# The second group's weight sums queued one group later, their rows 4 KB

## The chip, the cores and the metric

The kernel runs on one core of a Trainium2 chip. A core has a tensor engine (PE, whose weight loads the profile lists as PEld), a vector engine (DVE), a scalar engine (ACT), a general engine (POOL, GpSimd) and a sync engine (SP) that here only issues transfers. Sixteen DMA engines move the data. The metric is the device time of one execution, in microseconds (us), as the median of several runs.

## What is computed

One transformer block on 1024 positions of width 1024, all in fp32: a mixer (stick-breaking attention beside a gated linear recurrence) and an MLP with a squared relu. The change touches how the MLP's weights are prepared.

```python
def sq_relu_mlp(h, w_up, w_down):
    return jnp.square(jax.nn.relu(h @ w_up)) @ w_down

def reference(x, norm1_g, w_in, ..., norm2_g, w_up, w_down):
    h = rms_norm(x, norm1_g[l])
    x = x + hybrid_mixer(h, w_in[l], ..., w_out[l])
    h = rms_norm(x, norm2_g[l])
    x = x + sq_relu_mlp(h, w_up[l], w_down[l])
```

`w_up` is 1024 x 4096 and `w_down` 4096 x 1024.

## The kernel before

Each fp32 matmul is made of three matmuls on operands split in a high and a low part (`mmc`, L633): ACT rounds the high part (`split`, L544), DVE or POOL subtracts it from the operand (`lo_part`, L60). So each operand tile costs a pass of ACT and one of DVE or POOL before PE can use it.

The program has three parts in time. First the input projections, the recurrence and attention, whose pieces stand in a list, `ORDER`. Then the output projection with the second norm. Then the MLP, in two groups of 2048 hidden units: `up_group(0)`, `down_group(0)`, `up_group(1)`, `down_group(1)` (L837). In each, matrix products of 2 x 2 blocks are made with seven block products in place of eight (Winograd's form of Strassen's scheme): `p1` to `p7`. This needs sums of weight blocks. A group of the MLP has 14 products of 96 matmuls, 1344 in all.

In `up_group(g)` the first loop over j (`a` tiles, one load for each j) makes two block products in one go. A loop on `rs` tiles follows (`p6` and `p7`; POOL adds two loaded halves, L698), then one on `rt` tiles (`p4`; one load for two j, first operand `t4`), then one on `ru` and `rv` tiles: four loads for each j, and POOL adds them (L737). I call this last loop the `ru` loop. In `down_group(g)` a product runs over four k. It loads one tile for each k, `p1`, `p3`, `p7` and `p2`, or two that POOL adds (`rp`, `qp`, L767), `p5`, `p6` and `p4`. Before each product some tiles of the activations `U` are combined, on POOL or DVE (`s1` to `s4`, L798 to L817). The order of the products is p1, p5, p6, p3, p7, p2, p4.

The sums that several steps share are made by DMA, from DRAM to DRAM. `weight_sum(n)` (L136) copies 2 MB of `w_up` or `w_down` to a half of `sum_u` or `sum_d` (n % 4 of 0 or 1), or adds 2 MB to it on the way (`accum_op`, n % 4 of 2 or 3; called an accumulate below, the other a plain copy). There are 16: n = 0 to 3 and 4 to 7 for `sum_u` and `sum_d` of group 0, queued in attention (the Y entries of `ORDER`), 8 to 11 and 12 to 15 for those of group 1, queued in `up_group(0)` and `down_group(0)`. All are issued by POOL, in line with its arithmetic: what stands behind such an issue on POOL comes after it.

What fixes the order: the program is built with a scheduler that simulates the time of each instruction and chooses from it each engine's order (`schedule_with_timeline_sim=True`, L870). At run time each engine works its list in order. `issue_after(marked[0])` keeps a sum behind the POOL addition that was last marked with `mark`. The loads go through six `raws` buffers (`raw`, L529), so a load waits till the tile six before it has been used. The consumers of group 1's sums are the loads of `SU` (L697, L735, L736) and of `SD` (`rd`, L792).

Of the kernel before, what the change touches and what calls it, by code (L numbers as in the profile page):

```python
# [14 lines left out]
ALU = mybir.AluOpType  # L15
# [28 lines left out]
def kernel(ctx, tc, x, norm1_g, w_in, conv_w, conv_b, w_rg, b_rg, w_ig, b_ig,  # L44
                             lam, q_norm_g, k_norm_g, w_out, norm2_g, w_up, w_down, out):
    nc = tc.nc
# [89 lines left out]
    def weight_sum(n):  # L136
        m, g = (("u", 0), ("d", 0), ("u", 1), ("d", 1))[n // 4]
        i, k, dst = ((1, 0, 0), (0, 1, 1), (0, 0, 0), (1, 1, 1))[n % 4] if m == "u" else ((1, 1, 0), (0, 0, 1), (0, 1, 0), (1, 0, 1))[n % 4]

        def rows(w):  # L140
            return w.rearrange("j p c -> (j p) c") if len(w.shape) == 3 else w


        f = 16 * g + 8 * i
        src = rows(w_up[k, f:f + 8] if m == "u" else w_down[k, f * P:(f + 8) * P])
        with tc.issue_after(marked[0]):
            nc.gpsimd.dma_start(rows(sums[m, g][dst]), src, max_dma_last_dim=2048, **({"accum_op": ALU.add} if n % 4 > 1 else {}))

    left1 = ExitStack()
    hp = pool(left1, "hT")  # L150
# [493 lines left out]
    def up_group(g):  # L644
# [25 lines left out]
        for j in range(9):  # L670
            cur = None
            if j < 8:
                st = station(f"a{g}{j}", two(w_up[:, 16 * g + j]))
                ps = out_bank(f"p1_{g}{j}")
                mm4(ps, st, 0, b11)
                nc.scalar.copy(U[:, j, 2], ps)
                cur = (ps, st)
            if held is not None:
                ps, st = held
                mm4(ps, st, 1, b21, False)  # L680
                relu2(j - 1, 0, ps)
            held = cur

        for u in range(2):
# [9 lines left out]
        for j in range(8):  # L694
            r = raw(f"rs{g}{j}")
            nc.sync.dma_start(r[:, 0], w_up[1, 16 * g + 8 + j])
            nc.sync.dma_start(r[:, 1], SU[0, j])  # L697
            mark(nc.gpsimd.tensor_tensor(r[:, 0], r[:, 0], r[:, 1], **add))  # L698
            if g == 0 and j % 4 == 0:
                weight_sum(8 + j // 4)  # L700
            st = split(nc.vector, pair(stp, f"s{g}{j}"), r)
            ps = out_bank(f"p6_{g}{j}")
            mm4(ps, st, 0, t2)
            nc.vector.tensor_tensor(U[:, j, 2], U[:, j, 2], ps, **sub)
            ps = out_bank(f"p7_{g}{j}")
            mm4(ps, st, 1, t3)
            nc.vector.tensor_tensor(U[:, j, 3], ps, U[:, j, 2], **add)
# [4 lines left out]
            nc.vector.tensor_tensor(r, hb(1, 0, u), hb(1, 1, u), **sub)  # L712
            t4.append(split(lo_eng(), pair(mvp, f"t4{g}{u}"), r))
        for j in range(8):
            if g == 0 and j % 4 == 2:
                weight_sum(10 + j // 4)
            if j % 2 == 0:
                st = station(f"t{g}{j}", two(w_up[1, 16 * g + 8 + j:16 * g + 10 + j]))
            ps = out_bank(f"p4_{g}{j}")
            mm4(ps, st, j % 2, t4)  # L720
            nc.vector.tensor_tensor(U[:, j, 1], ps, U[:, j, 3], **sub)  # L721
            relu2(j, 1)
# [30 lines left out]
    def down_group(g):  # L753
        SD = sums["d", g]

        def banks4(q, name):
            return [bank(q[t], [512], f"{name}{g}{t}") for t in range(4)]

        def product(name, pss, src, unit, start):

            for k in range(0, 8, 2):
                r = raw(f"r{name}{g}{k}")
                nc.sync.dma_start(r, src[0](k))
                if len(src) > 1:
                    q = raw(f"q{name}{g}{k}")
                    nc.sync.dma_start(q, src[1](k))
                    mark(nc.gpsimd.tensor_tensor(r, r, q, **add))  # L767
                    if g == 0 and name != "p4" and k % 4 == 0:
                        weight_sum(12 + (2 if name == "p6" else 0) + k // 4)
                mv = split(nc.vector, pair(mvp, f"{name}{g}{k}"), r)  # L770
                st = split(nc.vector if len(src) > 1 else lo_eng(), pair(stp, f"{name}{g}{k}"), unit(k))
                for a in range(2):
                    for t in range(4):
                        c = slice(t * P, t * P + P)
                        mmc(pss[t], st[0][:, a, c], st[1][:, a, c], mv[0][:, a], mv[1][:, a], start and k + a == 0, k + a == 7)

        def acc(pss, rows, n, scale, last=False):

            for t in range(4):
                r = 4 * rows + t  # L780
                xs = x1[:, r, 512 * n:512 * n + 512]
                nc.vector.scalar_tensor_tensor(xs, pss[t], scale[:, r:r + 1], xs, op0=ALU.mult, op1=ALU.add)
                if last and g == 1:
                    nc.sync.dma_start(out[r * P:(r + 1) * P, 512 * n:512 * n + 512], xs)

        def wd(i, n):
            def src(k):
                f = (16 * g + 8 * i + k) * P
                return w_down[n, f:f + 2 * P].rearrange("(a p) c -> p a c", p=P)
            return src  # L790

        def rd(i):  # L792
            return lambda k: SD[i, k * P:(k + 2) * P].rearrange("(a p) c -> p a c", p=P)

        def unit(q):
            return lambda k: U[:, k:k + 2, q]

        def s1(k):  # L798
            u = U[:, k:k + 2]
            (nc.gpsimd, nc.vector)[k // 2 % 2].tensor_tensor(u[:, :, 2], u[:, :, 2], u[:, :, 3], **sub)  # L800
            return u[:, :, 2]

        def s2(k):
            u = U[:, k:k + 2]
            (nc.gpsimd, nc.vector)[k // 2 % 2].tensor_tensor(u[:, :, 2], u[:, :, 2], u[:, :, 0], **sub)
            return u[:, :, 2]

        def s4(k):
            u = U[:, k:k + 2]
            r = raw(f"s4{g}{k}")  # L810
            mark(nc.gpsimd.tensor_tensor(r, u[:, :, 1], u[:, :, 2], **add))
            return r

        def s3(k):
            u = U[:, k:k + 2]
            nc.vector.scalar_tensor_tensor(u[:, :, 2], u[:, :, 2], -1.0, u[:, :, 3], op0=ALU.mult, op1=ALU.subtract)
            return u[:, :, 2]  # L817

        pa = banks4(QA, "pa")
        product("p1", pa, (wd(0, 0),), unit(0), True)  # L820
        acc(pa, 0, 0, rs2)
        pb = banks4(QB, "pb")
        product("p5", pb, (wd(0, 0), wd(0, 1)), s1, True)
        acc(pb, 1, 1, rs2)
        product("p6", pa, (rd(0), wd(0, 0)), s2, False)
        acc(pa, 0, 1, nrs2)
        product("p3", pb, (wd(1, 1),), s4, False)
        acc(pb, 0, 1, rs2, True)
        product("p7", pa, (rd(0),), s3, False)
        acc(pa, 1, 1, nrs2, True)  # L830
        pc = banks4(QB, "pc")
        product("p2", pc, (wd(1, 0),), unit(1), True)
        acc(pc, 0, 0, rs2, True)
        product("p4", pa, (rd(0), rd(1)), unit(3), False)
        acc(pa, 1, 0, rs2, True)
# [39 lines left out]
```

## Time and profile before

| | before |
|---|---|
| median of 3 runs | 1215.21 us (1215.03 to 1216.63) |
| the profiled execution | 1218.14 us, of which 1216.4 us are its span |
| PE busy | 1150.6 us, 95% |
| DVE, ACT, POOL busy | 897.3, 568.5, 586.5 us |
| granted clock of PE, mean | 0.969 |
| moved by DMA | 157.05 MB, mean 129 GB/s |

Queue q1 carries SP's loads and stores, q0 the weight sums that POOL issues:

```profile
q1 hardware_dynamic: 79040, 122.54, 30.5%
q0 software_dynamic: 12544, 33.56, 11.8%
```

The columns are packets, MB and the share of the sixteen DMA engines' time. The group lines give for each kind of issue its number, size and median time from issue to landing, in us; the sums are the largest transfers:

```profile
sum_u<-in_w_up_dram POOLq DMA_DIRECT2D x8, 2048.0 KB, 12.7
sum_d<-in_w_down_dram POOLq DMA_DIRECT2D x8, 2048.0 KB, 13.3
rp<-in_w_down_dram SPq DMA_DIRECT2D x32, 512.0 KB, 4.1
rp<-sum_d SPq DMA_DIRECT2D x24, 512.0 KB, 5.4
```

Three rows of PE's timeline place the parts: a product of the gates in attention (`pgl`) at 200.76, where the order of attention begins to differ below; the first matmul of the output projection (`po`), so the end of attention; and the first matmul of the MLP. A row has start, length, engine, line, operation, operands, and in brackets PE's idle time before it and what ended it.

```profile
200.76 0.79 PE L71 MATMUL pgl<-hTh,wl_gl 128*128 128x512 f32 x1 [1.99 <-DVE gx L487]
466.02 0.80 PE L71 MATMUL po<-sh_o,mix0l 128*128 128x512 f32 x1 [4.98 <-DVE mix0l L60]
566.29 0.79 PE L633 MATMUL p<-mh_b,sl_a 128*128 128x512 f32 x1 [4.00 <-DVE sl_a L60]
```

### The profile page before, as it was taken

Reading aid. Unit: us, or ns where it says so; the run is one execution under the profiler, and the core shown is the slowest. Engines: PE = TensorE matmul, PEld = TensorE weight load, DVE = VectorE, ACT = ScalarE, POOL = GpSimd, SP = SyncE. Lnnn points to the kernel's source line nnn. Section 1 sums busy time; section 2 is a strip of 40 time slices with the busy share of each in tenths; the row PEclk is TensorE's granted clock in tenths of the full one; section 3 lists DMA queues with packets and bytes.
Section 4 is the critical chain, followed back from the end, with each engine's and each line's share of the span. In section 5 each row is a group of like instructions: output and inputs, shape, how many; then the busy total and the mean of one; then the engine's idle time right before and its main releaser. Section 6 shows DMA issues by size and latency. Waiting matters only on the chain.

```text
span 1216.4 us, 15273 instructions
## 1 busy us (share of the span) xinstructions
PE 1150.6 (95%) x5410; PEld 948.0 (78%) x5410; DVE 897.3 (74%) x1182; ACT 568.5 (47%) x991; POOL 586.5 (48%) x472
## 2 busy tenths in 40 slices
PE   7998899999999988998999989889999999999998
PEld 7976777789987766886888767678887887878887
DVE  6889997999898788226387769685843876699663
ACT  7554475665665564144433554233334335733331
POOL 1356764574355566102645746533317368483240
PEclk9999999799999978998999989989999999999999
DMA  8110026824505275200453788944412345442531
GB/s 262 48 49 35 18 96 130 227 66 145 122 5 112 89 256 181 101 1 35 141 188 130 201 241 287 224 142 139 141 35 87 122 144 191 158 148 73 193 132 69
DMA packets 91659, 157.05 MB, mean 129 GB/s; under 512 B 8848, under 2 KB 27328, under 8 KB 91584
## 3 DMA queue, kind: packets, MB, share of 16 engines
q1 hardware_dynamic: 79040, 122.54, 30.5%
q0 software_dynamic: 12544, 33.56, 11.8%
q8 instruction: 42, 0.69, 0.2%
q14 instruction: 33, 0.27, 0.1%
HBM read 145.58 MB, written 44.04 MB: 156 GB/s over the span
## 4 chain that ended last, share of the span: by engine, by line
PE 69%; DVE 13%; issue 8%; DMA 3%; POOL 3%; ACT 3%; SPq 0%; DVEq 0%; ACTq 0%; POOLq 0%
PE p L633 22%; PE pa L633 11%; PE pb L633 5%; PE pc L633 4%; PE pd L71 3%; PE pd L72 3%; PE pd L73 3%; PE po L71 3%; PE po L72 2%; PE po L73 2%; PE av L461 2%; PE z L432 2%; PE pw L452 2%; DVE g L441 2%; DVE sl_u L60 2%
## 5 line engine op out<-in xcount | busy, mean ns | idle before, releaser
L442 POOL TENSOR_TENSOR w<-w,g 128x128 f32<-128x128 f32 (+3 forms) x96 | 99.7, 1044 | 107.7 <-DVE g L441 52.7
L60 DVE TENSOR_TENSOR ml_p<-rp,mh_p 128x1024 fp32r<-128x1024 f32 x56 | 110.3, 1971 | 28.1 <-ACT mh_p L544 28.1
L441 DVE TENSOR_TENSOR_SCAN g<-g 128x128 f32<-128x128 f32 (+3 forms) x96 | 112.6, 1185 | 8.0 <-ACT g L436 5.4
L544 ACT CAST sh_p<-U 128x1024 fp32r<-128x1024 f32 x48 | 50.5, 1051 | 131.0 <-PE pa L633 59.2
L633 PE MATMUL pa<-mh_p,sl_p 128*128 128x512 f32 x256 | 100.7, 393 | 7.1 <-DVE sl_p L60 6.8
L767 POOL TENSOR_TENSOR rp<-rp,qp 128x1024 f32<-128x1024 f32 x24 | 69.0, 2876 | 70.3 <-DMA qp<-in_w_down_dram 39.8
L633 PE MATMUL pa<-ml_p,sh_p 128*128 128x512 f32 x256 | 100.3, 392 | 0.0
L633 PE MATMUL pa<-mh_p,sh_p 128*128 128x512 f32 x256 | 100.1, 391 | 0.0
L71 PE MATMUL pd<-wh_p,hTl 128*128 128x384 f32 x256 | 90.9, 356 | 7.3 <-DVE vv L206 5.0
L72 PE MATMUL pd<-wl_p,hTh 128*128 128x384 f32 x256 | 89.8, 351 | 0.1
L73 PE MATMUL pd<-wh_p,hTh 128*128 128x384 f32 x256 | 88.3, 345 | 0.0
L60 DVE TENSOR_TENSOR sl_p<-U,sh_p 128x1024 fp32r<-128x1024 f32 x38 | 63.4, 1668 | 30.7 <-ACT sh_p L544 30.7
L737 POOL TENSOR_TENSOR ru<-ru,rv 128x1024 f32<-128x1024 f32 x16 | 43.8, 2769 | 58.9 <-DMA rv<-sum_u 58.8
L544 ACT CAST mh_p<-rp 128x1024 fp32r<-128x1024 f32 x56 | 58.7, 1048 | 21.3 <-POOL rp L767 14.6
L633 PEld LDWEIGHTS pa<-mh_p,sl_p 128*128 128x128 f32 x256 | 48.5, 189 | 18.2 <-DVE sl_p L60 7.5
L662 POOL TENSOR_TENSOR U<-U 128x512 f32<-128x512 f32 x32 | 47.0, 1501 | 32.0 <-ACT U L660 32.0
L456 ACT CAST wth<-pw 128x512 fp32r<-128x512 f32 (+1 forms) x80 | 42.4, 545 | 38.0 <-PE pw L452 24.8
L436 ACT ACTIVATE g<-z 128x384 f32<-128x384 f32 (+3 forms) x96 | 47.8, 497 | 22.9 <-PE z L434 10.4
L71 PEld LDWEIGHTS pd<-wh_p,hTl 128*128 128x128 f32 x256 | 49.4, 193 | 11.0 <-DVE vv L206 6.7
L660 ACT ACTIVATE U<-U 128x512 f32<-128x512 f32 x48 | 30.0, 628 | 58.6 <-DVE U L721 31.1
L60 DVE TENSOR_TENSOR wtl<-pw,wth 128x512 fp32r<-128x512 f32 (+1 forms) x80 | 49.5, 629 | 9.5 <-ACT wth L456 8.9
L633 PEld LDWEIGHTS pa<-mh_p,sh_p 128*128 128x128 f32 x256 | 48.5, 189 | 10.2
(325 smaller groups left out, 3566.7 us busy)
## 6 DMA issues: line engine op xcount, KB each, us to landing
sum_u<-in_w_up_dram POOLq DMA_DIRECT2D x8, 2048.0 KB, 12.7
sum_d<-in_w_down_dram POOLq DMA_DIRECT2D x8, 2048.0 KB, 13.3
rp<-in_w_down_dram SPq DMA_DIRECT2D x32, 512.0 KB, 4.1
rp<-sum_d SPq DMA_DIRECT2D x24, 512.0 KB, 5.4
ra<-in_w_up_dram SPq DMA_DIRECT2D x16, 512.0 KB, 4.4
qp<-in_w_down_dram SPq DMA_DIRECT2D x16, 512.0 KB, 4.2
wr_p<-in_w_in_dram SPq DMA_DIRECT2D x24, 192.0 KB, 5.8
xt<-in_x_dram SPq DMA_DIRECT2D x8, 512.0 KB, 7.5
```

Source lines behind the costliest of these rows:

```text
L60: ins = eng.tensor_tensor(lo, src, hi.bitcast(F32), op=ALU.subtract)
L71: nc.tensor.matmul(ps, al, bh, start=start, stop=False)
L72: nc.tensor.matmul(ps, ah, bl, start=False, stop=False)
L73: nc.tensor.matmul(ps, ah, bh, start=False, stop=stop)
L436: nc.scalar.activation(g[:, :kn], z, AF.Sigmoid, scale=-1.0)
L441: nc.vector.tensor_tensor_scan(gr, gr, gr, g[:, kn:kn + 1], op0=ALU.mult, op1=ALU.bypass)
L442: mark(nc.gpsimd.tensor_tensor(w[:, :kn], w[:, :kn], g[:, 1:kn + 1], op=ALU.mult))
L544: nc.scalar.copy(hl[0], src)
L633: nc.tensor.matmul(ps, x_, y_, start=start and n == 0, stop=stop and n == 2, skip_group_check=True)
L662: mark(nc.gpsimd.tensor_tensor(c, c, c, op=ALU.mult))
L737: mark(nc.gpsimd.tensor_tensor(r, r, q, **add))
L767: mark(nc.gpsimd.tensor_tensor(r, r, q, **add))
```

## The change

Two things change. `rows` views the 2 MB of a sum as 512 rows of 4 KB in place of 1024 of 2 KB, for all 16 sums, and the cap on a row is raised with it. And the eight sums for group 1 are queued elsewhere. Those of `sum_u` (8 to 11) leave `up_group(0)` for the start of the four products of `down_group(0)` that load one tile at a time (`steps`: p1, p3, p7, p2). Those of `sum_d` (12 to 15) leave `down_group(0)` for `up_group(1)`: two in the first loop at j = 2 and 6, one in the `rs` loop at j = 2, one at the start of the `p4` loop.

```diff
-            return w.rearrange("j p c -> (j p) c") if len(w.shape) == 3 else w
+            return (w.rearrange("j p c -> (j p c)") if len(w.shape) == 3 else w.rearrange("f c -> (f c)")).rearrange("(a b) -> a b", b=1024)
...
-            nc.gpsimd.dma_start(rows(sums[m, g][dst]), src, max_dma_last_dim=2048, **({"accum_op": ALU.add} if n % 4 > 1 else {}))
+            nc.gpsimd.dma_start(rows(sums[m, g][dst]), src, max_dma_last_dim=4096, **({"accum_op": ALU.add} if n % 4 > 1 else {}))
...
                 relu2(j - 1, 0, ps)
+                if g == 1 and j in (2, 6):
+                    weight_sum(12 + j // 4)
...
             mark(nc.gpsimd.tensor_tensor(r[:, 0], r[:, 0], r[:, 1], **add))
-            if g == 0 and j % 4 == 0:
-                weight_sum(8 + j // 4)
+            if g == 1 and j == 2:
+                weight_sum(14)
...
         for j in range(8):
-            if g == 0 and j % 4 == 2:
-                weight_sum(10 + j // 4)
+            if g == 1 and j == 0:
+                weight_sum(15)
...
                     mark(nc.gpsimd.tensor_tensor(r, r, q, **add))
-                    if g == 0 and name != "p4" and k % 4 == 0:
-                        weight_sum(12 + (2 if name == "p6" else 0) + k // 4)
                 mv = split(nc.vector, pair(mvp, f"{name}{g}{k}"), r)
                 st = split(nc.vector if len(src) > 1 else lo_eng(), pair(stp, f"{name}{g}{k}"), unit(k))
+                if g == 0 and k == 0 and name in steps:
+                    weight_sum(8 + steps.index(name))
...
+        steps = ("p1", "p3", "p7", "p2")
         pa = banks4(QA, "pa")
```

The order that the scheduler makes of it differs in these places. In the rows below a name carries the group and the step (`rp602` is the `rp` tile of p6, group 0, k = 2; `ru03` that of group 0, j = 3), and the last column is the shape.

First POOL in the down group of group 0, around p6, before:

```order
L767 TENSOR_TENSOR rp504_7499<-rp504_7499,qp504_7501 128x1024
L147 DMA sum_d1_96<-in_w_down_dram 1024x512
L767 TENSOR_TENSOR rp506_7538<-rp506_7538,qp506_7540 128x1024
L60 TENSOR_TENSOR sl_p106_7387<-U_6149,sh_p106_7386 128x1024
L805 TENSOR_TENSOR U_6149<-U_6149 128x2x512
L767 TENSOR_TENSOR rp600_7580<-rp600_7580,qp600_7582 128x1024
L147 DMA sum_d1_96<-in_w_down_dram 1024x512
L767 TENSOR_TENSOR rp602_7619<-rp602_7619,qp602_7621 128x1024
L767 TENSOR_TENSOR rp604_7657<-rp604_7657,qp604_7659 128x1024
L147 DMA sum_d1_96<-in_w_down_dram 1024x512
L805 TENSOR_TENSOR U_6149<-U_6149 128x2x512
L811 TENSOR_TENSOR s400_7746<-U_6149 128x1024
```

And now, up to the next sum:

```order
L769 TENSOR_TENSOR rp600_7575<-rp600_7575,qp600_7577 128x1024
L807 TENSOR_TENSOR U_6149<-U_6149 128x2x512
L769 TENSOR_TENSOR rp602_7613<-rp602_7613,qp602_7615 128x1024
L769 TENSOR_TENSOR rp604_7651<-rp604_7651,qp604_7653 128x1024
L769 TENSOR_TENSOR rp606_7689<-rp606_7689,qp606_7691 128x1024
L807 TENSOR_TENSOR U_6149<-U_6149 128x2x512
L813 TENSOR_TENSOR s400_7739<-U_6149 128x1024
L147 DMA sum_u1_94<-in_w_up_dram 512x1024
L813 TENSOR_TENSOR s402_7776<-U_6149 128x1024
```

The last of `sum_d` stood ahead of the second `U` step (L805) and of `s400`; both now stand ahead of the sum. The other sums of this group go behind p5's first addition and the split after it, behind `s406`, and between p4's additions `rp402` and `rp404`.

Then POOL in the up groups. In that of group 0, where two accumulates stood behind `ru02` and `ru04`, there is no sum any more. In that of group 1, where none stood, these rows are of the first loop and the `rs` loop now:

```order
L662 TENSOR_TENSOR U_6149<-U_6149 128x512 x2
L147 DMA sum_d1_96<-in_w_down_dram 512x1024
L60 TENSOR_TENSOR sl_a14_8464<-ra14_8461,sh_a14_8463 128x1024
L662 TENSOR_TENSOR U_6149<-U_6149 128x512
L700 TENSOR_TENSOR rs10_8634<-rs10_8634 128x512
L700 TENSOR_TENSOR rs11_8670<-rs11_8670 128x512
L662 TENSOR_TENSOR U_6149<-U_6149 128x512 x2
L147 DMA sum_d1_96<-in_w_down_dram 512x1024
L60 TENSOR_TENSOR sl_a17_8567<-ra17_8564,sh_a17_8566 128x1024
L700 TENSOR_TENSOR rs12_8706<-rs12_8706 128x512
L147 DMA sum_d1_96<-in_w_down_dram 512x1024
```

The first two sums are plain copies, the third, two rows behind the second, is an accumulate. The last one of the program stands ahead of the `ru` loop of group 1:

```order
L739 TENSOR_TENSOR ru10_9106<-ru10_9106,rv10_9107 128x1024
L60 TENSOR_TENSOR ml_t411_8932<-t4r11_8929,mh_t411_8931 128x1024
L147 DMA sum_d1_96<-in_w_down_dram 512x1024
L60 TENSOR_TENSOR ml_t111_9093<-h2_5424,mh_t111_9092 128x1024
L739 TENSOR_TENSOR ru11_9133<-ru11_9133,rv11_9134 128x1024
```

There `ml_t411` is the low part of p4's second operand. With the sums PE's rows for j = 4 and 5 of group 1's first loop change places.

Last PE in attention, where no line of code changes. Before, at about 200 us (`pgl` is a product of the gates, `av` and `pw` belong to attention):

```order
L452 MATMUL pw0032_1641<-ident_79,w007512_1594 128x128
L461 MATMUL av003_1614<-wtl0030_1621,vv0_289 128x256
L461 MATMUL av003_1614<-wth0030_1620,vv0_289 128x256
...
L233 MATMUL pk12_2432<-identr_84,ks12_2416 128x128 x4
L71 MATMUL pgl01_3097<-hTh_100,wl_gl0_0_2787 128x512
L72 MATMUL pgl01_3097<-hTl_101,wh_gl0_0_2786 128x512
```

And now:

```order
L452 MATMUL pw0032_1641<-ident_79,w007512_1594 128x128
L71 MATMUL pgl01_3097<-hTh_100,wl_gl0_0_2787 128x512
L72 MATMUL pgl01_3097<-hTl_101,wh_gl0_0_2786 128x512
...
L73 MATMUL pgl01_3097<-hTh_100,wh_gl0_5_2816 128x512
L461 MATMUL av003_1614<-wtl0030_1621,vv0_289 128x256
```

Eighteen matmuls of the gate's product moved ahead of `av003`. From there to the end of attention rows of all engines are shifted against each other, on PE by at most 65 places; in the output projection and the MLP, but for the places above, a few rows change.

## The prediction

> **What bounds the kernel now.** I read first the busy shares: the tensor engine (PE) is busy for 1150.6 of 1216.4 us, so time can only be won where PE waits or runs at a low clock. Since the MLP does the same work twice (group 0, then group 1, 1344 matmuls each), the second view cuts the span into the same three stretches of each group. Its columns are the stretch, busy us and instruction count of PE, weight load, DVE, ACT and POOL, then the granted clock, the DMA share and GB/s. Two slices of attention stand ahead.
>
> ```profile
> 220.00:240.00 20.00, 18.01 (x84) 13.61 (x83) 18.41 (x28) 12.07 (x30) 10.40 (x20) 0.77 0.94 214
> 240.00:260.00 20.00, 20.00 (x99) 16.01 (x97) 18.16 (x22) 13.10 (x29) 16.47 (x16) 0.80 0.42 132
> 566.29:680.00 113.71, 113.70 (x493) 94.01 (x494) 71.80 (x69) 44.61 (x57) 63.19 (x34) 0.97 0.46 149
> 680.00:800.00 120.00, 102.98 (x424) 82.59 (x424) 93.52 (x61) 50.78 (x65) 69.27 (x32) 0.93 0.85 232
> 800.00:899.01 99.01, 99.01 (x439) 82.00 (x437) 65.59 (x54) 36.09 (x36) 30.85 (x11) 1.00 0.38 128
> 899.01:1000.00 100.99, 99.82 (x440) 82.24 (x439) 60.91 (x49) 38.27 (x47) 49.25 (x26) 1.00 0.32 104
> 1000.00:1110.00 110.00, 105.78 (x455) 86.08 (x455) 90.48 (x62) 55.69 (x71) 75.58 (x30) 0.98 0.46 154
> 1110.00:1210.40 100.40, 100.40 (x444) 83.14 (x443) 59.32 (x52) 31.25 (x32) 25.82 (x10) 1.00 0.35 121
> ```
>
> Group 0 takes 113.71 + 120.00 + 99.01 = 332.7 us, group 1 311.4. What they do not share is the weight sums for group 1, which run under group 0 alone. The chain of waits gives PE's full pace, and its last steps the worst stall (start, length, what):
>
> ```profile
> 768.78 12.19 issue
> 780.98 0.07 POOL sum_d L147
> 781.05 0.75 issue
> 781.80 2.91 POOL U L805
> 784.71 2.35 POOL s L811
> ...
> 787.08 0.04 DVE U L816
> 787.12 3.24 issue
> 790.36 3.38 DVE sl_p L60
> 793.74 0.04 issue
> 793.78 18.35 PE pa L633 x72
> 812.13 21.76 PE pb L633 x96
> ```
>
> 96 matmuls take 21.76 us, 0.2267 each. So 680 to 800 holds 424 x 0.2267 = 96.1 us of work and loses 23.9; the like stretch of group 1, 1000 to 1110, holds 103.1 and loses 6.9. **The difference is 17.0 us**, and it is the price of the sums where they stand now: the other two stretches differ mainly by the start of the MLP, which the change doesn't touch.
>
> The chain says how. POOL does nothing for 12.19 us ahead of the last sum's issue, then makes the two tiles that PE is waiting for. The timeline of POOL shows the sums (idle time before, in brackets), and the queue rows of the same trace what they move (packets, MB, share of the sixteen engines' time in the window: 593 to 603, then 676 to 696.5, then 763 to 780.9):
>
> ```profile
> 611.37 0.78 POOL L147 DMA_DIRECT2D sum_u<-in_w_up_dram  x1
> 675.68 1.35 POOL L147 DMA_DIRECT2D sum_u<-in_w_up_dram  x1
> 696.56 1.30 POOL L147 DMA_DIRECT2D sum_u<-in_w_up_dram  x1 [8.83 <-issue]
> 726.81 0.80 POOL L147 DMA_DIRECT2D sum_d<-in_w_down_dram  x1
> 780.98 1.31 POOL L147 DMA_DIRECT2D sum_d<-in_w_down_dram  x1 [12.19 <-issue]
> ```
>
> ```profile
> q0 software_dynamic: 528, 2.10, 62.6%
> q0 software_dynamic: 1040, 2.10, 56.0%
> q0 software_dynamic: 1040, 2.10, 64.0%
> ```
>
> A plain copy is already 528 packets (0.80 us of POOL, 62.6% of 10 us or 6.3 us of the engines); an accumulate is 1040 (1.30 us, 56.0% of 20.5 us or 11.5 us). Both long idles are an accumulate behind an accumulate: the second is issued just when the first has moved its last packet, and POOL stands meanwhile. These are PE's waits that follow, and the slices around them:
>
> ```profile
> 686.89 0.50 PE L633 MATMUL p<-mh_t,sl_u 128*128 128x512 f32 x1 [2.37 <-DVE sl_u L60]
> 707.99 0.80 PE L633 MATMUL p<-mh_t,sl_u 128*128 128x512 f32 x1 [5.59 <-DVE sl_u L60]
> 736.49 0.50 PE L633 MATMUL p<-mh_b,sl_u 128*128 128x512 f32 x1 [1.08 <-DVE U L741]
> 793.78 0.79 PE L633 MATMUL pa<-mh_p,sl_p 128*128 128x512 f32 x1 [6.78 <-DVE sl_p L60]
> 1090.82 0.61 PE L633 MATMUL pb<-mh_p,sl_p 128*128 128x512 f32 x1 [2.01 <-DVE sl_p L60]
> ```
>
> ```profile
> 600.00:620.00 20.00, 20.00 (x90) 16.54 (x90) 10.28 (x6) 10.38 (x13) 14.84 (x10) 1.00 0.66 215
> 680.00:700.00 20.00, 17.63 (x71) 14.04 (x71) 15.18 (x11) 9.02 (x14) 11.06 (x9) 0.91 0.92 217
> 700.00:720.00 20.00, 14.41 (x55) 11.48 (x54) 13.79 (x9) 7.17 (x11) 9.26 (x4) 0.83 1.03 274
> 780.00:800.00 20.00, 13.22 (x51) 10.44 (x51) 12.92 (x10) 4.83 (x5) 14.90 (x6) 0.83 0.71 150
> 860.00:880.00 20.00, 20.00 (x90) 16.55 (x89) 16.00 (x13) 8.01 (x8) 6.05 (x2) 1.00 0.43 139
> 1000.00:1020.00 20.00, 19.32 (x85) 15.68 (x85) 13.29 (x10) 9.08 (x13) 20.00 (x12) 1.00 0.57 191
> 1080.00:1100.00 20.00, 17.99 (x72) 14.38 (x71) 20.00 (x12) 7.81 (x8) 14.72 (x6) 0.91 0.29 106
> ```
>
> Each wait is paid twice: the clock falls behind it. The slices lose (1 - 0.91) x 20 = 1.8, 3.4 and 3.4 us to the clock in group 0. With the waits (2.37 + 5.59 + 6.78 = 14.7) that makes 23.3 of the 23.9.
>
> **The change part by part.**
>
> *Taken out of group 0.* Two plain sums leave p6 of the up group, where nothing was lost (90 matmuls in the slice from 600, with a sum in flight). Two accumulates leave the steps around 675 to 697, with the stall of 8.83, and the four of `sum_d` leave p5 and p6 of the down group, with the stall of 12.19. If group 0 then runs as group 1 does now, 17.0 us go. What is late next there is what is late in group 1: the wait of 2.01 behind DVE, which is busy for all 20.00 us of that slice. That is inside the 6.9 that I leave.
>
> *Put into group 0's down group.* One plain copy stands after p5's first addition, just where the first sum of `sum_d` stood at 726.81; the stretch that I compare with has none. Bounds: nothing, and one wait like the 2.01 with its 1.8 of clock, 3.8. I take 0.5, near nothing, since PE's wait there now, at 736.49, is 1.08. One plain copy and one accumulate go behind the first and the last `s4` tile, one accumulate into p2. POOL gives each 0.8 to 1.3 us, and is busy 6.05 of 20 us from 860. PE has 90 matmuls in that slice, its full number, at a DMA share of 0.43: 0 us. Three transfers add at most 6.3 + 11.5 + 11.5 = 29.3 us of engine time to a stretch of 99 us at 0.38, so the share stays near 0.68, like the 0.66 of the slice from 600 that lost nothing.
>
> *Put into group 1's up group.* Two plain copies and an accumulate enter its first 50 us: share 0.32 now, at most 24.1 us more in a stretch of 101, so 0.56, again 0 us. The third follows the second with two instructions between them on POOL, so it may stand there till the second is out, up to 6.3 us. Queued behind it are squares and additions for p6, which are made well ahead: cover is there for that wait. The last accumulate goes behind the second operand of p4, right ahead of the steps in which group 0 was hurt: POOL is busy all 20.00 us from 1000, so 0.8 to 1.3 us of issue count in full, and the loads of those steps share the engines with it. Bounds: 0 and the 2.37 + 1.8 = 4.2 that the first accumulate cost at 686.89. I take 2.0, the middle, since it stands behind the first of the eight `ru` additions, where that one stood behind the third.
>
> *Rows of 4 KB.* They change nothing for the plain copies (528 packets already). For accumulates 1040 packets become about 528: POOL 0.5 us less for each of eight. The engines' time lies between 6.3 us (a plain copy of the same packets) and 11.5 (the bytes are the limit); I reckon with 11.5 above, so a lower one only adds cover. On the path: 0.
>
> *The order of attention.* Its eight sums have the same places in the list, but shorter issues made the scheduler shift PE's rows by up to 65 places from about 200 to 466 us. That stretch has its own waits. Bounds from its largest loss, the two slices quoted first, (0.23 + 0.20) x 20 = 8.6 us of clock: one such stretch gone, -8.6; one more, +8.6. I see no reason for a side: 0.
>
> Sum: -17.0 + 0.5 + 2.0 = **-14.5 us**. The profiled execution took 1218.14 us (span 1216.4 and 1.7 around it), so 1203.6 by its own measure; it lies 2.9 us over the median 1215.21, so I expect a median of 1215.2 - 14.5 = 1200.7, say **1201**.
>
> A rule speaks on the clock: the Trainium skill, "TensorE: Matmul & The Clock Gate", Part 1 (the HAM clock gate), has the clock fall after an idle window of about 3.4 us. The waits of 2.37 and 2.01 us are shorter, and still the granted share fell to 0.91 in their slices, so the trace disagrees. By the page what group 0 keeps would be 2.0 rather than 3.8 and the sum -16.3; I go by the rows.
>
> **The rivals.**
>
> 1. *The stall moves one group on.* The last accumulate meets the loads of group 1's steps and costs what its two forerunners cost together, 2.37 + 5.59 + 1.8 + 3.4 = 13.2, in place of 2.0: -3.3, about 1212. For it: POOL's 20.00 of 20. Against: only one transfer is there, so none waits behind another. Beside this stands a rule of the Trainium skill ("DMA: Bandwidth & Descriptors", Issuing engines are not separate DMA queues): all queues run on the same sixteen engines and interleave, so a moved transfer takes its share wherever it goes. The DMA shares of 0.92 and 1.03 agree.
> 2. *The loads alone hold group 0.* Half of the 17.0 stays: -6, about 1209. Against: the same loads in group 1 run at a share of 0.46.
> 3. *Attention gets better.* A low-clock stretch like 220 to 260 goes: -23.1, about 1192.
> 4. *Attention gets worse, and the kernel slower.* The new order breaks PE's feed so that low-clock stretches of 8.6 come in: with one, 1209; with two, 17.2 is more than the 14.5 won, and the time is 1218. That is the point from which it decides.
> 5. *The change doesn't do what it says:* accumulates stay at 1040 packets, and the one in p6 holds POOL behind the copy ahead. The cover above takes that: 0 to 2 us, 1201 to 1203, inside my forecast.
>
> **How the numbers follow.** Forecast (1195 to 1207) 0.60; below 1195 (rival 3) 0.10; 1207 to 1212.8 (rivals 1 and 2, one bad stretch of 4) 0.16; around 1212.8 to 1217.6 (rival 1 with some of 4) 0.07; above (rival 4) 0.07. I call 0.2% what a measurement of this kernel can tell, 2.4 us. So faster 0.86, same 0.07, slower 0.07. The range, 1191 to 1212, leaves out some 0.05 below and 0.15 above.
>
> **What would show it.** Right: no idle of POOL over 3 us ahead of a sum; 680 to 790 with some 7 us lost and a DMA share near 0.5; group 0 near 316 us and group 1 near 313; accumulates of 528 packets. Wrong: a wait over 5 us in group 1's steps near 1000, with an accumulate in flight (rival 1); group 0's waits unchanged though POOL is free (rival 2); the end of attention, 466 now, moved by over 5 us (3 and 4).

## The result, and the profile after

The change is **slower**: 1228.72 us median of 4 runs (1225.2 to 1229.45) against 1215.12 of the kernel before beside it (1214.32 to 1216.63). The ratio is 1.0105, with a 95% interval of 1.0083 to 1.0126, so 10 to 15 us are lost where 14.5 were to be won.

Four times of PE's timeline divide the profiled execution: the start of the output projection (`po`), of the MLP, of group 1, and the span's end. A row has start, length, engine, line, operation, operands, and in brackets PE's idle time before it and what ended it. These are those rows of the changed kernel, with its longest waits between them:

```profile
202.00 0.79 PE L71 MATMUL pgl<-hTh,wl_gl 128*128 128x512 f32 x1 [4.93 <-DVE gx L487]
240.54 0.48 PE L452 MATMUL pw<-ident,w 128*128 128x128 f32 x1 [4.07 <-DVE wtl L60]
476.02 0.80 PE L71 MATMUL po<-sh_o,mix0l 128*128 128x512 f32 x1 [4.91 <-DVE mix0l L60]
576.47 0.80 PE L633 MATMUL p<-mh_b,sl_a 128*128 128x512 f32 x1 [4.00 <-DVE sl_a L60]
716.80 0.80 PE L633 MATMUL p<-mh_t,sl_u 128*128 128x512 f32 x1 [5.72 <-DVE sl_u L60]
777.97 0.79 PE L633 MATMUL pb<-mh_p,sl_p 128*128 128x512 f32 x1 [3.38 <-DVE sl_p L60]
900.96 0.39 PE L633 MATMUL p<-mh_b,sl_a 128*128 128x512 f32 x1
1041.22 0.79 PE L633 MATMUL p<-mh_t,sl_u 128*128 128x512 f32 x1 [5.29 <-DVE sl_u L60]
```

Attention ends at 476.0 in place of 466.0. Group 0 takes 900.96 - 576.47 = 324.5 in place of 332.7, group 1 from there to the end of the span (1227.2) 326.2 in place of 317.4. So the three shares are **+10.0, -8.2 and +8.8**; the forecast had 0, -16.5 and +2.0.

The windows put a reason under each. Columns as before: stretch, busy us and count of PE, weight load, DVE, ACT and POOL, granted clock, DMA share, GB/s. First attention from 180 on, in the kernel before and then in the changed one:

```profile
180.00:466.02 286.02, 268.35 (x1471) 220.39 (x1469) 245.35 (x433) 171.99 (x404) 154.97 (x209) 0.93 0.46 126
```

```profile
180.00:476.02 296.02, 267.76 (x1479) 219.57 (x1477) 253.82 (x438) 170.23 (x404) 156.63 (x209) 0.93 0.45 123
```

PE is busy for the same time at the same clock (268.35 and 267.76 us, 0.93). It only waits more: 286.02 - 268.35 = 17.7 us before, 28.3 now. Then the stretches of group 0 and group 1 of the changed kernel where the forecast looked:

```profile
690.18:810.18 120.00, 110.82 (x463) 90.29 (x462) 93.85 (x68) 55.12 (x69) 74.19 (x31) 0.94 0.52 168
...
1001.95:1111.95 110.00, 100.85 (x429) 81.95 (x429) 80.80 (x57) 53.75 (x69) 74.35 (x31) 0.97 0.54 167
```

In group 0 PE waits 9.2 of 120 us (17.0 before), and the DMA share fell from 0.85 to 0.52. In group 1 it waits 9.1 of 110 (4.2 before), at a DMA share of 0.54 (0.46 before). The sums themselves went as the diff says: the queue moves the same bytes in fewer packets, and POOL's timeline shows no idle time ahead of any of the 16.

```profile
q0 software_dynamic: 8448, 33.56, 11.3%
```

So POOL's long idles are gone, the DMA engines are less loaded in group 0, and PE still waits over 5 us in the `ru` loop, in both groups. The chain of waits of the changed kernel shows how (start, length, what), group 0 and then group 1:

```profile
707.27 4.35 DMA rp<-in_w_down_dram
...
711.64 1.05 ACT mh_p L544
...
715.54 1.22 DVE sl_u L60
```

```profile
1031.73 5.97 DMA rp<-in_w_down_dram
...
1037.73 1.05 ACT mh_p L544
...
1039.94 1.23 DVE sl_u L60
```

`mh_p` is the rounding of the first tile of `p1`, the product that comes *after* the loop. It stands in ACT's list ahead of `sh_u05`, which PE needs now. ACT's timeline shows the price, in the changed kernel's group 0 and 1 and, last, in group 1 before:

```profile
711.64 1.04 ACT L544 CAST mh_p<-rp 128x1024 fp32r<-128x1024 f32 x1 [6.39 <-DMA rp<-in_w_down_dram]
712.60 1.04 ACT L544 CAST sh_u<-ru 128x1024 fp32r<-128x1024 f32 x1
...
1037.73 1.04 ACT L544 CAST mh_p<-rp 128x1024 fp32r<-128x1024 f32 x1 [7.54 <-DMA rp<-in_w_down_dram]
```

```profile
1027.51 1.05 ACT L544 CAST mh_p<-rp 128x1024 fp32r<-128x1024 f32 x1 [1.00 <-DMA rp<-in_w_down_dram]
```

The same order cost 1.00 us in group 1 before. DVE's line has the same order: the low part of that tile (`ml_p`) stands ahead of the low part that PE waits for (`sl_u`). In the changed kernel's group 0 it took 2.89 us between ACT's row and `sl_u`, in group 1 1.23:

```profile
712.72 2.89 DVE L60 TENSOR_TENSOR ml_p<-rp,mh_p 128x1024 fp32r<-128x1024 f32 x1 [4.71 <-ACT mh_p L544]
```

SP issues the load of `rp` right behind a load of `rv` that has to wait for an addition on POOL to free its `raws` buffer: in group 0 the addition ends at 703.93 + 2.39 = 706.32, that load is issued at 706.36 and `rp`'s at 707.27. This is 707.27 - 576.47 = 130.8 us into group 0 and 130.8 into group 1; in group 1 before it was 1023.63 - 899.01 = 124.6. In group 1 the loads that meet the last accumulate hold the additions up: POOL idles 4.25 us for `rv` in the changed kernel, and has no idle at this place before (the accumulate was issued at 993.14).

```profile
1010.54 2.85 POOL L739 TENSOR_TENSOR ru<-ru,rv 128x1024 f32<-128x1024 f32 x1 [4.25 <-DMA rv<-sum_u]
```

For attention, DVE's timeline shows the same thing with another load. Before, and then in the changed kernel:

```profile
194.50 0.39 DVE L467 TENSOR_TENSOR ob<-av,ot 64x256 f32<-64x256 f32 x1
194.82 0.13 DVE L439 COPY g<-g 128x1 f32<-128x1 f32 x1
194.88 0.67 DVE L60 TENSOR_TENSOR wtl<-pw,wth 128x512 fp32r<-128x512 f32 x1
195.48 1.26 DVE L441 TENSOR_TENSOR_SCAN g<-g 128x512 f32<-128x512 f32 x1
200.02 0.69 DVE L487 TENSOR_TENSOR gx<-pgl,gx 128x512 f32<-128x512 f32 x1 [3.27 <-DMA gx<-rs_d]
```

```profile
201.26 0.69 DVE L487 TENSOR_TENSOR gx<-pgl,gx 128x512 f32<-128x512 f32 x1 [5.87 <-DMA gx<-rs_d]
201.87 0.40 DVE L467 TENSOR_TENSOR ob<-av,ot 64x256 f32<-64x256 f32 x1
202.20 0.13 DVE L439 COPY g<-g 128x1 f32<-128x1 f32 x1
202.26 0.67 DVE L60 TENSOR_TENSOR wtl<-pw,wth 128x512 fp32r<-128x512 f32 x1
202.85 1.26 DVE L441 TENSOR_TENSOR_SCAN g<-g 128x512 f32<-128x512 f32 x1
```

The load of `gx` is late in both (the chain has 7.48 us for it before, 7.91 now, with an accumulate on the engines: the sums' queue had 94.8% of their time from 192.5 to 199.5 before, 82.3% from 193 to 201 now). But four rows of DVE, `wtl0031` for attention among them, now stand behind the row that needs it, and on PE the gate's product, which waits for that row, stands ahead of `av003`. DVE idles 5.87 us, and PE 4.93. The Trainium skill ("TensorE: Matmul & The Clock Gate", Architectural detail, on engine queue depths) has ACT and DVE as strict first-in first-out queues; these rows agree: ACT idled 6.39 us though the operand of the `sh_u` behind was ready at 706.32, and DVE 5.87 us though that of `wtl0031` was ready at 195.56, early in that idle.

### The profile page after: what moved, and what is told of

Same layout as the page of the kernel before. It is cut to its first block, busy times and chain, and to the rows that moved or that the text cites. A ratio compares the mean times of both kernels' runs of the same rounds, so it can differ in the third digit from the quotient of the medians.

```text
span 1227.2 us, 15265 instructions
## 1 busy us (share of the span) xinstructions
PE 1152.0 (94%) x5410; PEld 950.3 (77%) x5410; DVE 894.4 (73%) x1182; ACT 567.6 (46%) x991; POOL 588.8 (48%) x472
## 4 chain that ended last, share of the span: by engine, by line
PE 74%; DVE 13%; issue 5%; DMA 3%; ACT 3%; POOL 1%; SPq 0%; DVEq 0%; ACTq 0%; POOLq 0%
PE p L633 24%; PE pa L633 12%; PE pb L633 5%; PE pc L633 4%; PE pd L71 3%; PE pd L72 3%; PE pd L73 3%; PE po L71 2%; PE av L461 2%; PE po L72 2%; PE po L73 2%; PE pw L452 2%; DVE sl_p L60 2%; PE z L432 2%; DVE g L441 2%
## 5 line engine op out<-in xcount | busy, mean ns | idle before, releaser
L442 POOL TENSOR_TENSOR w<-w,g 128x128 f32<-128x128 f32 (+3 forms) x96 | 102.2, 1071 | 109.3 <-DVE g L441 67.8
L60 DVE TENSOR_TENSOR ml_p<-rp,mh_p 128x1024 fp32r<-128x1024 f32 x56 | 107.3, 1916 | 45.9 <-ACT mh_p L544 45.9
L633 PE MATMUL pa<-mh_p,sl_p 128*128 128x512 f32 x256 | 99.9, 390 | 0.1
L633 PE MATMUL pa<-ml_p,sh_p 128*128 128x512 f32 x256 | 99.7, 390 | 0.0
L633 PE MATMUL pa<-mh_p,sh_p 128*128 128x512 f32 x256 | 99.7, 390 | 0.0
L60 DVE TENSOR_TENSOR sl_p<-U,sh_p 128x1024 fp32r<-128x1024 f32 x38 | 71.3, 1877 | 28.2 <-ACT sh_p L544 28.1
L452 PE MATMUL pw<-ident,w 128*128 128x128 f32 x288 | 49.6, 294 | 10.4 <-DVE wtl L60 8.2
L633 PE MATMUL pb<-mh_p,sl_p 128*128 128x512 f32 x128 | 51.6, 403 | 7.3 <-DVE sl_p L60 7.3
L633 PE MATMUL p<-mh_b,sl_a 128*128 128x512 f32 x128 | 51.4, 406 | 6.3 <-DVE sl_a L60 6.3
L633 PEld LDWEIGHTS pa<-mh_p,sl_p 128*128 128x128 f32 x256 | 48.1, 188 | 10.7 <-POOL sl_p L60 0.5
## 6 DMA issues: line engine op xcount, KB each, us to landing
sum_u<-in_w_up_dram POOLq DMA_DIRECT2D x8, 2048.0 KB, 12.2
```

The costliest lines, as they stand in the source:

```text
L60: ins = eng.tensor_tensor(lo, src, hi.bitcast(F32), op=ALU.subtract)
L442: mark(nc.gpsimd.tensor_tensor(w[:, :kn], w[:, :kn], g[:, 1:kn + 1], op=ALU.mult))
L452: nc.tensor.transpose(pw[:, i * P:(i + 1) * P], wrow[rr][j // 4][:, j % 4 * P:(j % 4 + 1) * P], ident)
L633: nc.tensor.matmul(ps, x_, y_, start=start and n == 0, stop=stop and n == 2, skip_group_check=True)
```

## The experiments

The theory after these traces (A) had two parts. *Order*: with shorter issues in attention the scheduler makes another order, and that order alone costs the 10 us. *Line*: in the MLP the places are a gain, of which ACT's standing in line for `rp` takes half back. The rivals were that the packets of 4 KB cost something in themselves, and that the moved sums load POOL or the engines whatever ACT does. All kernels, in the order in which they were run; "po", "g0" and "g1" are the start of the output projection and the two groups' times, read as above from each profiled execution. Each ratio is to the kernel before run beside it (medians 1215.12 to 1218.07). A profiled execution can lie off its kernel's median: by 5.4 us above it in `places_only_order_kept`, by 4.8 below it in `rows_last8`, by less in the others.

| kernel | median us | ratio to before (95%) | po | g0 | g1 |
|---|---|---|---|---|---|
| before | 1215.12 | 1 | 466.0 | 332.7 | 317.4 |
| the change | 1228.72 | 1.0105 (1.0083 to 1.0126) | 476.0 | 324.5 | 326.2 |
| rows_plain_first8 | 1230.21 | 1.0112 (1.0079 to 1.0146) | 475.8 | 333.2 | 317.9 |
| rows_acc_first8 | 1217.44 | 1.0008 (0.9989 to 1.0028) | 465.3 | 335.7 | 317.9 |
| rows_last8 | 1207.92 | 0.9928 (0.9904 to 0.9952) | 456.0 | 326.1 | 318.1 |
| places_only_order_kept | 1211.15 | 0.9961 (0.9942 to 0.998) | 467.0 | 322.4 | 325.2 |
| last_sum_in_rs_loop | 1208.47 | 0.9926 (0.99 to 0.9952) | 464.3 | 321.8 | 321.6 |
| act_rounds_p1_late | 1198.17 | 0.9847 (0.9819 to 0.9875) | 461.1 | 316.2 | 318.2 |
| both_moves | 1200.91 | 0.9878 (0.9851 to 0.9904) | 463.9 | 315.5 | 319.5 |
| places_only_2kb | 1215.2 | 0.9979 (0.9955 to 1.0003) | 460.0 | 321.7 | 329.9 |
| change_act_late | 1210.49 | 0.9953 (0.993 to 0.9976) | 473.5 | 318.0 | 318.7 |
| before_act_late | 1210.75 | 0.9949 (0.9925 to 0.9973) | 463.8 | 325.0 | 316.1 |
| change_gate_pinned | 1222.22 | 1.0048 (1.002 to 1.0076) | 473.7 | 321.5 | 324.2 |
| change_gx_pinned | 1221.13 | 1.002 (1.0001 to 1.0039) | 468.4 | 325.3 | 325.8 |

### The rows alone, in three parts

The kernel before, with rows of 4 KB for some sums and no sum moved; only the condition differs.

```diff
+        wide = n < 8 and n % 4 < 2      # rows_plain_first8
+        wide = n < 8 and n % 4 > 1      # rows_acc_first8
+        wide = n >= 8                   # rows_last8
-            nc.gpsimd.dma_start(..., max_dma_last_dim=2048, ...)
+            nc.gpsimd.dma_start(..., max_dma_last_dim=4096 if wide else 2048, ...)
```

> The kernel before, with rows of 4 KB for the four plain copies of group 0's sums alone (n = 0, 1, 4, 5). These copies already moved in 528 packets, so the transfers stay what they were and only the order of attention changes (763 of PE's rows differ, against 775 in the changed kernel). Theory A, the new order of attention costs the 10 us by which its end slipped (466.0 to 476.0): the time is 1223 to 1227 and the output projection starts near 476. Theory B, the 4 KB packets of the accumulates hold the DMA engines longer and cost it: 1214 to 1217, projection near 466.

> The kernel before, with rows of 4 KB for the four accumulates of group 0's sums alone (n = 2, 3, 6, 7). No engine's order changes, the accumulates move in 528 packets of about 328 ns in place of 1040 of 176. Theory A (order): 1213 to 1217, the projection starts near 466. Theory B (packets): 1223 to 1227, near 476.

> The kernel before, with rows of 4 KB for the eight sums of group 1 alone, at their places of before; no engine's order changes. Theory A, an accumulate waits behind an accumulate for room that 2 x 1040 packets do not leave and 2 x 528 do: POOL's idle of 8.83 and 12.19 us goes, PE's wait of 6.78 and most of that of 5.59 with their clock (3.4 each) go, 1201 to 1207. Theory B, a second accumulate waits for the first whatever its rows: both idles stay over 6 us, 1212 to 1217.

`rows_plain_first8` moves the packets it moved before and changes only the order of attention, to nearly that of the change: 763 of PE's rows differ from before, in the change 775, and its waits of 4.48 us for `gx` at 199.16 and 4.45 at `pw` at 238.45 are the change's 4.93 and 4.07. (POOL's issue of such a copy is also 0.13 us shorter, 0.67 for 0.80.) It costs the whole loss of attention: po at 475.8, ratio 1.0112, and a median of 1230.21 where 1223 to 1227 us were expected. `rows_acc_first8` halves the packets of attention's accumulates, keeps the order, shortens POOL's issues too (1.05 us for 1.32), and costs nothing (po 465.3). So it is the order, not the packets. PE's waiting from 180 us to po says the same: 14.4 to 18.8 us in the nine profiled executions with the order of before, 28.3 to 29.5 in the three with the change's order or nearly that (the change, `rows_plain_first8`, `change_act_late`).

`rows_last8` was the surprise. With 528 packets for each accumulate POOL's idles of 8.8 and 12.2 us are gone at the *old* places, as theory A had it, and the kernel gains 0.7% (1207.92, just over that theory's 1201 to 1207). But the second accumulate is now issued into the first, and the `ru` loop's loads share the engines with both (from 679 to 696.7 the sums' queue has 69.9% of the engines' time, the loads' queue the rest). POOL's timeline, then the chain and PE's timeline of that kernel:

```profile
678.86 1.00 POOL L151 DMA_DIRECT2D sum_u<-in_w_up_dram  x1
...
696.79 2.34 POOL L741 TENSOR_TENSOR ru<-ru,rv 128x1024 f32<-128x1024 f32 x1 [9.79 <-DMA rv<-sum_u]
```

```profile
679.27 17.36 DMA rv<-sum_u
```

```profile
707.83 0.80 PE L637 MATMUL p<-mh_b,sl_u 128*128 128x512 f32 x1 [12.16 <-DVE U L745]
```

A stall of POOL became a wait for a load of 17.36 us (a load of `rp` took 3.85 in group 1 before), and PE's single longest wait of the study, 12.16 us.

### The places alone

The changed kernel with rows of 2 KB for n < 8, so that attention keeps the order of before (`wide = n >= 8`); and the same with 2 KB for all sixteen (`wide = False`).

> The changed kernel, with rows of 2 KB for the eight sums of group 0, so that attention has the order of before (no row of PE differs there). Theory A, the loss is the sum of attention's order (+10.2) and of two groups that about cancel (-8.2 and +8.8): 1213 to 1218, group 0 near 324 us from its first matmul to group 1's, PE's wait of about 5 us in both ru loops again. Theory B, attention's end only shifts what comes later and the groups adapt: 1223 to 1229 all the same.

> The new places with all sixteen sums in rows of 2 KB, attention as before. Theory A (the long idles of POOL come only of two accumulates of 1040 packets in flight together, and at the new places no two meet): no idle over 3 us ahead of a sum, and the median equal to places_only_order_kept within 2.5 us, 1209 to 1214. Rival B (rows of 4 KB are what frees POOL at the new places too): an idle of 8 to 13 us ahead of the third or the last sum of group 1, and 1215 to 1222.

The places gain a little, 0.9961. With `rows_plain_first8` the parts add to 1.0112 x 0.9961 = 1.0073, near the 1.0105 of the change. With 2 KB everywhere no idle of POOL comes back either, as theory A has it: no accumulate is issued into another. The median is 4.0 us above the other's, where at most 2.5 were expected, and its profiled execution has a wait of 2.95 us in the `rs` loop of group 1 that the other doesn't have. But the two intervals overlap, so that difference stays open.

### Taking the wait out of the `ru` loop, two ways

Both are built on `places_only_order_kept`. The first moves the last accumulate one loop ahead; the second holds ACT's rounding of `p1`'s first tile, and with it DVE's low part of that tile, behind the last tile of the `ru` loop and moves no sum; the third does both.

```diff
-            if g == 1 and j == 2:
-                weight_sum(14)
+            if g == 1 and j in (2, 6):          # last_sum_in_rs_loop
+                weight_sum(14 + j // 4)
...
-        nc.scalar.copy(hl[0], src)
+        rounded.append(nc.scalar.copy(hl[0], src).ins)          # act_rounds_p1_late
...
-                mv = split(nc.vector, pair(mvp, f"{name}{g}{k}"), r)
+                with tc.issue_after(rounded[-1]) if name == "p1" and k == 0 else ExitStack():
+                    mv = split(nc.vector, pair(mvp, f"{name}{g}{k}"), r)
```

> Built on places_only_order_kept (1211.2), with the last accumulate one loop earlier, behind the seventh addition of the rs loop of group 1, so it should be out before the loads of the ru loop. Theory A (the last accumulate delays the ru loop's loads, and POOL's additions with them): group 1's wait of 4.8 us and its low-clock slice of 3.4 go, group 1 falls from 325 to about 318, the median to 1203 to 1206. Rival B (POOL's own queue makes the wait, whatever is in flight): the wait stays over 4 us, group 1 at 324 to 326, the median at 1210 to 1212. Rival C (the accumulate meets the one before it and POOL stands still for some 10 us): an idle of POOL ahead of the sum and a new wait in the rs loop, 1212 to 1220.

> Built on places_only_order_kept (1211.2); ACT rounds p1's first tile only after the last tile of the ru loop, in both groups, and no sum moves. Theory A (ACT stands in line for the load of rp, with sh_u05 to sh_u07 queued behind it, and PE waits for those): group 0's wait of 5.6 us and the clock behind it (3.4) go, group 0 falls from 322 to 313 to 316; group 1's 4.8 and 3.4 go too for the most part, for there ACT stands in line for the same load; the median 1196 to 1204. Rival B (POOL's additions are late by themselves, so that PE waits for U or for the ru tiles anyway): the waits move by one or two tiles and stay over 4 us, 1209 to 1212. Rival C (p1 then starts late): a wait of 3 to 6 us ahead of p1's first matmul takes the place of each, 1209 to 1214.

> Both edits of the two runs beside this one. If each takes away a wait of its own: the sum of the two gains, but group 1's wait counted once, so 1195 to 1202, group 0 at 313 to 316 and group 1 at 316 to 318. If both only act on the same wait in group 1 (Theory A for the accumulate alone): no better than the better of the two by over 2 us.

Either edit removes the wait of 4.8 us in the `ru` loop of group 1. With the sum gone from there, ACT's timeline and PE's in `last_sum_in_rs_loop` read

```profile
1019.38 1.05 ACT L548 CAST mh_p<-rp 128x1024 fp32r<-128x1024 f32 x1 [1.03 <-DMA rp<-in_w_down_dram]
```

```profile
1025.16 0.50 PE L637 MATMUL p<-mh_t,sl_u 128*128 128x512 f32 x1 [1.07 <-DVE sl_u L60]
```

which is that loop as it was before (1.00 of ACT and 1.06 of PE there), and POOL's idle for `rv` falls from 3.38 us in `places_only_order_kept` to 0.27. The gain is smaller than forecast (group 1 at 321.6, not 318; the median 1208.47, not 1203 to 1206). By medians it isn't shown: the interval overlaps that of `places_only_order_kept`. Group 0 keeps its 5.6 us, as it must. `act_rounds_p1_late` takes both waits, and it is the **fastest kernel of the study: 1198.17 us, 0.9847 (0.9819 to 0.9875)** of before. Its windows of the two stretches show it (L639 there is L633):

```profile
675.90:795.90 120.00, 114.72 (x495) 94.13 (x494) 100.15 (x72) 55.58 (x69) 75.05 (x31) 0.97 0.58 184
...
979.37:1089.37 110.00, 105.99 (x464) 86.50 (x464) 89.15 (x63) 55.51 (x72) 75.80 (x32) 1.00 0.53 172
```

PE waits 5.3 and 4.0 us where the change waits 9.2 and 9.1, at a better clock. Rival C (`p1` starts late) is not seen: no wait over 1 us stands in the `ru` loop or ahead of `p1`. Both edits together are no better than ACT's alone (1200.91 against 1198.17, overlapping intervals), as expected if they act on one wait.

### The line on ACT without the places, and the change with it

The same edit on ACT, on the kernel before and on the change as it is.

> The kernel before, with that one edit on ACT and no sum moved. Theory A (the gain of act_rounds_p1_late needs both: the sums out of group 0's ru loop, and ACT's order): the wait of 5.6 us at 702 and its clock 3.4 go or shrink, for the load of rp is not in ACT's line any more, but POOL's idles of 8.8 and 12.2 stay with the waits of 2.4 and 6.8; 1205 to 1212. Rival B (the edit on ACT alone does it, the places of the sums are worth nothing): 1197 to 1202. Rival C (in the kernel before, the waits come of POOL alone): 1214 to 1217.

> The change as it is (1228.7), with ACT's rounding of p1's first tile held behind the last tile of the ru loop. Theory A (two separate causes: the order of attention costs some 13 us by medians, ACT's place in line some 13 more): output projection still begins at 473 to 478, group 0 at 316 and group 1 at 318 as in act_rounds_p1_late, the median 1211 to 1217, no better than before. Rival B (attention's loss was made up of what follows it, or varies by itself): 1198 to 1206, the output projection at 461 to 468.

On the kernel before it gains 0.5%, and the wait at about 700 stays (5.32 us; 5.59 before), where theory A had it go or shrink. There ACT waits for POOL, which stands in the idle ahead of an accumulate; ACT's and POOL's timelines of `before_act_late`:

```profile
699.11 1.05 ACT L546 CAST sh_u<-ru 128x1024 fp32r<-128x1024 f32 x1 [2.73 <-POOL ru L739]
```

```profile
693.37 1.30 POOL L147 DMA_DIRECT2D sum_u<-in_w_up_dram  x1 [8.39 <-issue]
```

The other idle of POOL is 9.61 us there. Where the 0.5% comes from was not tested. The two edits give more together than their sum: the places alone win 0.4%, ACT alone 0.5%, both 1.5%. On the whole change the edit on ACT gives 318.0 and 318.7 for the groups, the MLP's full gain, and po still at 473.5: the order of attention takes most of that back, and 0.9953 is left, where no gain over before was expected.

### Which row of attention's order

Two edits on the change. The first puts PE's rows back (the gate's product behind `av003`), the second DVE's (`gx00` behind `wtl0031`); with the second the scheduler puts PE's `av003` ahead of the gate's product again as well.

```diff
+        with tc.issue_after(avs[0, 0, 3]) if (c, ch) == (0, 1) else ExitStack():      # change_gate_pinned
+            pd = proj_cols(gw[c // 2 * 2], c % 2, ch, f"pgl{c}{ch}")
...
+        with tc.issue_after(lows[0, 0, 3, 1]) if (c, ch) == (0, 0) else ExitStack():  # change_gx_pinned
+            nc.vector.tensor_tensor(y, pd, y, op=ALU.mult)
```

> The change as it is (1228.7), with the eighteen matmuls of the gate's product held behind av003, as they stood before. The scheduler then makes a third order of attention, which differs from the change's by 892 rows of PE and from before's by 721. Theory A (the one move of the gate's product makes the two waits of 4.9 and 4.1 us at 197 and 236, and these most of the 10 us): both fall under 2.5 us, the output projection begins at 466 to 470, the median 1218 to 1222. Rival B (the loss is spread over the whole order): one or both go, but the output projection still begins at 473 to 479, the median 1225 to 1232. MLP in both as in the change: 324 and 326.

> The change as it is (1228.7), with DVE's first product of the gate (gx00, which needs a load) held behind wtl0031, so that three of the four rows that stood ahead of it before stand ahead of it again; the scheduler makes a fourth order of the rest of attention. Theory A (PE's wait of 4.9 us at 197 is DVE standing in line for that load, with wtl0031 queued behind): DVE's idle ahead of gx00 falls from 5.9 to 4 to 5, PE's wait there from 4.9 to 1.7 to 2.6, with some 1.7 us less of low clock. Rival B (PE itself needs the load that early, whatever stands in DVE's line): the wait stays at 4.5 to 5. For the whole, if the waits of 4.1 at 236 and those after 430 stay: 1223 to 1227; if they go with it: 1216 to 1221.

DVE's and PE's timelines with PE's rows put back:

```profile
198.45 0.69 DVE L491 TENSOR_TENSOR gx<-pgl,gx 128x512 f32<-128x512 f32 x1 [5.70 <-DMA gx<-rs_d]
```

```profile
199.52 0.58 PE L463 MATMUL av<-wtl,vv 128*128 128x256 f32 x1 [5.06 <-DVE g L441]
```

and with DVE's:

```profile
198.43 0.69 DVE L491 TENSOR_TENSOR gx<-pgl,gx 128x512 f32<-128x512 f32 x1 [4.39 <-DMA gx<-rs_d]
```

```profile
199.17 0.65 PE L72 MATMUL pgl<-hTh,wl_gl 128*128 128x512 f32 x1 [2.49 <-DVE gx L491]
```

With the gate's product behind `av003` PE waits 5.06 us all the same, now for `av`, since DVE still stands at `gx`, with `ob` and `wtl0031` behind it (`ob` ends at 199.06 + 0.41 = 199.47, `av` starts at 199.52; the profile names the short row `g` that ends beside it). With DVE's rows back too the wait halves, 5.06 to 2.49. Theory A of the second run holds for this wait, and that of the first falls for it. What DVE's rows alone would do under the change's order of PE no run shows.

By medians both win back about half of the loss or more (1.0048 and 1.002, the change 1.0105), the first without touching this wait; its 1222.22 us lies between the ranges of its two theories. So it is a part of the loss only. PE's waiting up to po is 23.9 and 24.6 us with the two edits, 28.3 in the change and 17.7 before. Of that the waits at `pw` for `wtl` are 8.2 us in the change and 8.3 in `rows_plain_first8`, but 1.4 before and 1.7 and 1.8 with the two edits. In the change the chain to the largest of them, 4.07 us at 240.54, runs over a load of `wr_p` of 4.91 us and the rounding of it (`wh_p`) that stands ahead of `wth` on ACT: the same kind of line, but no run tests it. Both edits made a third and a fourth order of what follows, with waits of their own (3.12 us at 240.8 and 2.98 at 326.8 in the one, 3.28 at 230.8 in the other), so which rows make the rest of the loss stays open.

## Why the prediction was wrong, step by step

- **The order of attention, "I see no reason for a side: 0"** is the step that turned the sign. By medians it costs 1.1%, some 14 us (`rows_plain_first8`), more than its upper bound of 8.6 us. Two things failed. The bound was taken from clock losses, while the loss came as waits (17.7 us to 28.3) at an unchanged clock (0.93). And there was a reason for a side in the rows of DVE, which the step did not read: a row that needs a load of 7.48 us, on which DVE idled 3.27 us already, had moved ahead of four rows, and PE waits for some of them. That this row makes a part of the loss is shown, the rest of it is open. Rival 4 had the right side and kind ("breaks PE's feed"), but a price in low clock and a chance of 0.07.
- **"If group 0 then runs as group 1 does now, 17.0 us go"** failed by half: -8.2 in the change. What was late next was not the wait of 2.01 behind DVE but ACT, in line for `rp`, with DVE behind it. Group 1 had this order too, at 1.00 us; it was not in the sum because its load came 6 us sooner. That POOL is later in group 0 for an addition on `h` (L689, 3.40 us at 677.22), which group 1 does not have there, is only argued. With ACT's rounding held back, group 0 falls from 332.7 to 316.2: 16.5, as the first two terms added up to, but by an edit that the forecast did not have.
- **The last accumulate ahead of the `ru` loop, +2.0, at most 4.2.** Group 1 lost 8.8 in all. By the profiles the accumulate's place alone is 3.6 of it (325.2 to 321.6 in `last_sum_in_rs_loop`), and the line on ACT 7.0 (to 318.2), for the most part the same wait. Place and mechanism were named (rival 1: the loads of those steps share the engines with it); the bound lacked what stands behind the load, ACT's line. Without that line group 1 is at 318.2, +0.8, inside the bounds.
- **Plain copies, the accumulates behind `s4` and in `p2`, 0.5 and 0:** nearly right as far as the waits show. Two are longer there: the 3.38 at 777.97 (2.01 at the same place in group 1 before), and 2.29 us at 922.50, behind the first plain copy in group 1 (1.17 at 919.46 before). Neither was tested by itself.
- **Rows of 4 KB: 0 on the path, 11.5 us of the engines for an accumulate.** The upper bound was about right. The queue's row of the changed kernel for 991 to 1010, around one accumulate (packets, MB, share of the engines' time):

```profile
q0 software_dynamic: 528, 2.10, 57.4%
```

  That is 57.4% of 19 us, 10.9. The step missed that fewer packets free POOL at the old places (`rows_last8`), so that the idles which the forecast meant to remove by moving the sums needed no move (though a wait for loads of 12.16 us came in their place).

## What to carry to other kernels

Where a change shifts a scheduler's order, read the rows of the engines that feed PE as well as PE's: for each row that waits for a load, list what stands behind it in that engine's line and who waits for that; here one row of DVE was worth 2.6 us of PE's wait (5.06 to 2.49), and one of ACT with its row of DVE 13 us of the median. A stretch that is to run "as the other one does" has the other's luck in it, so compare when its loads are issued and what stands in line for them. And test the order apart from the transfers: an edit that left the packets as they were and changed the order showed the whole loss of attention in one run.

## What was not expected of the hardware

An accumulate of 2 MB in 528 packets takes the engines hardly less than one in 1040 (10.9 and 11.5 us), so halving its packets won little; a plain copy of 2 MB in 528 took 6.3, and what makes the difference no run takes apart. The Trainium skill ("Perfetto Trace Analysis", DMA Optimizations) says that larger transfers, 4 KB for 2 KB say, can dramatically improve throughput; for this one the runs show 5%. What the packets do change is POOL: issuing an accumulate into an accumulate of 1040 packets held it for 8.4 to 13.5 us in the four kernels with 2 KB there (eight issues), and not at all with 528 (`rows_last8`).

With one and the same order, attention's end lay between 456.0 and 467.0 us in the nine profiled executions that have the order of before. So 10 us of po in one profile can be the execution. That the new order costs is shown by the medians, and by the three profiles with the change's order or nearly that: they lie at 473.5 to 476.0, and PE waits at least 28.3 us in them, against at most 18.8 in the nine.
